# Modulation vectors of a two-layer transformer trunk: row blocks summed on VectorE, partitions on TensorE

## The chip, the cores and the metric

The kernel runs on one core of one Trainium2 chip. The metric is the device time of one execution in microseconds; the median of three runs is shown. "Modulation" means here what an adaptive norm takes from a conditioning vector: for each layer nine vectors of 1024 numbers (shift, scale and gate of three sublayers), for each of two streams.

## What is computed

Two layers work on 256 latent tokens (`x`) and 256 context tokens (`ctx`), 1024 features each. For both streams the same weights are used, but different modulation vectors, from `c` for `x` and from `c_ctx` for `ctx`:

```python
sc = jax.nn.silu(c)
scc = jax.nn.silu(c_ctx)
for l in range(DEPTH):
    mx = (sc @ w_ada[l] + b_ada[l]).reshape(bsz, N_MOD, 1, d)
    mc = (scc @ w_ada[l] + b_ada[l]).reshape(N_MOD, d)
    x = x + 0.5 * mx[2] * _swiglu(_modulate(_rmsnorm(x, norm_g[l, 0]), mx[0], mx[1]), w_ffn1_in[l], w_ffn1_out[l])
    ctx = ctx + 0.5 * mc[2] * _swiglu(...)
    hx = _modulate(_rmsnorm(x, norm_g[l, 1]), mx[3], mx[4])
    ...
    x = x + mx[5] * ox
    x = x + 0.5 * mx[8] * _swiglu(_modulate(_rmsnorm(x, norm_g[l, 2]), mx[6], mx[7]), w_ffn2_in[l], w_ffn2_out[l])
    if with_ctx:
        ctx = ctx + mc[5] * oc
        ...
return _rmsnorm(x, final_g)
```

`w_ada` is 1024 x 9216 for each layer, in fp32; the product with it is a matrix times two columns. The second layer's `ctx` is not needed behind the mixer, so of its modulations 5 to 8 only `x`'s part is used.

## The kernel before

All activations lie feature-major: eight tiles of 128 features by 512 tokens, `x` in the columns 0 to 255 and `ctx` in 256 to 511. Weights come from DRAM in blocks of 512 KB (`Unit`; four tiles of 128 rows by 256 columns), loaded by SP's queue into six buffers `wr`. ScalarE copies a block's high part into `wh` (L119), VectorE writes the rest into `wl` (L122, this pair is called the split), four buffers of each; TensorE then makes three products for each output tile and k (L110), so a block of two output tiles and four k with 512 tokens is 24 matmuls of 512 columns. A block has two parts, one for each output tile.

The feed-forward nets (FFN) take most blocks: pairs of "up" blocks (ScalarE applies silu) and "gate" blocks (VectorE multiplies from PSUM, ScalarE and VectorE split the product), then "down" blocks whose products VectorE adds to the tokens.

The modulation weights come as blocks of their own (`ada_units`, L272): for each modulation eight blocks of 128 rows by 1024 columns, called A blocks here. They are not split. `ada_product` (L242) multiplies a block with `sc` (the two silu vectors in the first two of 32 columns, one row block at a time) into one PSUM tile, in four matmuls of 256 columns, one for each group of 32 PSUM partitions; fp32 takes two instructions for each. At the eighth block VectorE turns 32x32 squares (L257), adds the bias (L122) and applies the norm's weight or the factor 0.5 into `mods`. The first two modulations of layer 0 are made in the opening (`first_ada`), with halves of 512 columns.

The program's order is written by hand. `mixed` (L1208) puts one A block behind each block of an FFN's middle: 56 in layer 0's first FFN (L1244), 56 of layer 1's in layer 0's second (L1248), eight in layer 1's first (L1250). The last eight (modulation 8 of layer 1) are `rest` (L1253): three between the last mixer output and the norm of the last FFN, the others behind every second block there (L1255). `ahead` (L1310) issues loads and splits for which there is room: a split up to four blocks ahead, a load when a `wr` buffer is over. `later` (L307) puts a function off by a number of parts. All engines run their queues in order.

Of the kernel before, what the change touches and what calls it, by code (L numbers as in the profile page):

```python
# [9 lines left out]
F32 = mybir.dt.float32  # L10
F32R = mybir.dt.float32r
U32 = mybir.dt.uint32
ACTF = mybir.ActivationFunctionType
ALU = mybir.AluOpType
# [3 lines left out]
KD = 8  # L18
# [6 lines left out]
# columns of w_mix_in  # L25
# [5 lines left out]
# columns of the float constants  # L31
# [3 lines left out]
N_STAGE, N_SPLIT = 6, 4  # weight blocks being loaded, and split  # L35
N_SLOT = 69
# of the layers' mixers: the turns between an attention item's stages, and the weights of the turns
# [8 lines left out]
class Ring:  # L46
    """Buffers of one size, handed out and given back in program order."""
# [22 lines left out]
class Unit:  # L70
    """A block of weights and the products that use it, in parts."""

    def __init__(self, src, shape, parts, split=True):
        self.src, self.shape, self.parts, self.split = src, shape, parts, split
        self.raw = self.hi = self.lo = None
        self.turned = 0  # the first columns' heads get the order (half, axis, frequency)
        self.far = False  # split far ahead, into buffers of the general ring


class Halves:  # L80
    """Two tiles of two k each, seen as one of four."""
# [14 lines left out]
def trunk_kernel(ctx: ExitStack, tc: tile.TileContext, a: dict, out: bass.AP, dbg=None):  # L96
# [11 lines left out]
    # ------------------------------------------------------------ helpers  # L108
# [3 lines left out]
    def mm3(o, lh, ll, rh, rl, start, stop):  # L112
        """(lh + ll)^T (rh + rl) in float32r passes."""
        mm(o, lh, rh, start, False)
        mm(o, lh, rl, False, False)
        mm(o, ll, rh, False, stop)
# [19 lines left out]
    # ---------------------------------------------------------- constants  # L136
# [5 lines left out]
    km = kf[:, C_TRI:C_TRI + 256].bitcast(U32)  # not 0 where a token counts  # L142
# [5 lines left out]
    nc.vector.memset(sc, 0.0)  # L148
    cols = [const.tile([128, 108], F32, name=f"cols{l}") for l in range(DEPTH)]
# [9 lines left out]
    # ------------------------------------------------------------- opening  # L159
# [41 lines left out]
    def tokens(k):  # L201
        """Tokens, feature-major: columns 0..255 are x, 256..511 are ctx."""
# [14 lines left out]
    def side_loads():  # L217
        """What only the mixers need."""
        nc.sync.dma_start(out=kf[:, 0:C_ID], in_=a["k_f"][:, 0:C_ID])
        for l in range(DEPTH):  # L220
# [13 lines left out]
            # minus lambda  # L234
# [4 lines left out]
    # ---------------------------------------------------------------- adaLN  # L239
    ada_ps = {}  # L240

    def ada_product(l, i, k, w, b0=0, nb=KD):  # L242
        """Row block k's share of modulation i of layer l, of the feature tiles b0.. (nb of them)."""
# [10 lines left out]
        if k < KD - 1:  # L254
            return
# [3 lines left out]
        m = mods[l][:, i, b0:b0 + nb]  # L259

        def wide(c0):
            c = cols[l][:, c0 + b0:c0 + b0 + nb]
            return c.rearrange("p (b o) -> p b o", o=1).to_broadcast([128, nb, 2])

        tt(m, tr[:, 0:32 * nb].rearrange("p (b r) -> p b r", r=32)[:, :, 0:2], wide(BADA + 8 * i), ALU.add)
# [5 lines left out]

    def ada_units(l, i):  # L272
        def part(k):
            return lambda u: ada_product(l, i, k, u.raw)
# [6 lines left out]
    def first_ada(b0):  # L281
        """Loads and products of what the first norm takes, for the feature tiles b0.. (4 of them)."""
# [14 lines left out]
    # ----------------------------------------------------------------- norm  # L297
# [9 lines left out]
    def later(f, parts=1):  # L307
        """Runs f after this many more parts: products whose operands are on their way."""
        put_off.append((n_part + parts, f))

    def square(m, c, x=None):
        """Adds tile m's squares in the columns c to the sums of squares."""
# [15 lines left out]
    def scale_of(c):  # L328
        """1 / rms of the tokens in the columns c."""
# [7 lines left out]
    def modulate(l, ni, ss, ks):  # L337
        """The tiles ks of the streams ss, normalised and modulated: all high parts, then the low ones."""
# [34 lines left out]
    def fm_units(w, c0, width, n, done, rh=None, kd=KD, r0=0, by_stream=False, turned=0):  # L373
        """Output features c0.. (128 or 256 of them), feature-major; done(m, psum, columns).

        by_stream: the parts are in two lists, x's and ctx's; done comes once for each when it is "twice".
        """
# [39 lines left out]
    def across(before, between, norm_of, after, n):  # L417
        """Units before a norm, the norm and units after it, stream by stream."""
# [29 lines left out]
    # ------------------------------------------------------------------ FFN  # L448
    def ffn(l, w_in, w_out, n, gi, after, by_stream=True):
        """Its first units, the others, the last ones and what follows these."""  # L450
# [51 lines left out]
    # ---------------------------------------------------------------- mixer  # L502
    def mixer(l, n):
        """n: the tokens that go on (512, or 256 when only x does)."""
# [11 lines left out]
        def rope(ps, nq):  # L516
            """Two heads, each in the order (half, axis, frequency): a turn pairs the rows p and p + 32."""
# [18 lines left out]
        def tm_units(c0, dst):  # L536
            """512 features, token-major."""
# [25 lines left out]
        def twice(dst, b, nq):  # L563
            """Each head of 64 in both halves of the partitions."""
# [11 lines left out]
        def bk_tokens():  # L576
            """Token-major keys of the GLA: [token, tile, head, 64]."""
# [43 lines left out]
        def gate_weights():  # L621
            """[rank of both directions and the bias, head, direction, 64]."""
# [14 lines left out]
        def r_done(b):  # L637
            def done(m, ps, c):
                # r sigmoid(r), with exp and ln only
# [12 lines left out]
        # ---- attention: items of stages, one stage a turn  # L652
# [13 lines left out]
        def head_norm(po, n, gcol, o, mul=None):  # L666
            """o = norm over the partitions of po, times gcol (and mul)."""
# [4 lines left out]
        def halves(q):  # L672
            """A tile of two 64s as two: [high; low] parts of the first, [low; high] of the second."""
# [8 lines left out]
        def doubled(k):  # L682
            """A tile of two 64s: for each its high part twice, and the low parts of both."""
# [9 lines left out]
        def score(o, q, m, c, kh, kl):  # L693
            """(high + low of q) high of k + high of q low of k"""
# [147 lines left out]
        def gla_items():  # L842
            items = []

            def decay(t):
                ts = slice(128 * t, 128 * t + 128)

                def s0():
                    # la: 16 times the log decays, [token, head, direction, 64]
# [31 lines left out]
            def head(h):  # L881
# [18 lines left out]
                def s1():  # L900
# [23 lines left out]
                    # the state each chunk starts from: [direction and key, chunk, value]  # L924
# [45 lines left out]
        def turns(items, lags=(0, 1, 2, 3)):  # L970
            """Turn t runs stage s of item t - lags[s], the oldest item first."""
# [13 lines left out]
        # ---- the merge  # L985
# [43 lines left out]
        def spread(units, groups):  # L1029
            """The groups' turns spread evenly over the units' parts.  # L1030

            groups: name -> (turns, weight of a turn); the units' list holds "may name" before which none of the
            group's turns may come, and "need name" by which all have come.
            """
# [52 lines left out]
        def send():  # L1087
            """The tokens wait in DRAM for their residual."""
# [42 lines left out]
        for cb in range(0, KD, 2):  # L1131
# [10 lines left out]
            else:  # the first halves of some blocks first: the last y come late  # L1142
# [26 lines left out]
    # ------------------------------------------------------------- the plan  # L1169
    fin = {"t": [], "xg": {}}  # L1170

    def to_out(m, c):
        """Tile m of the last residual: its squares, and itself back to token-major."""
# [34 lines left out]
    def mixed(units, fill, every=1):  # L1208
        """fill's items, one after each unit or after every so many."""
# [19 lines left out]
    # The first up-projection starts on the lower half of the features, while the others' modulation is loaded.  # L1229
# [37 lines left out]
    def split_unit(u, src, hi, lo):  # L1267
        """src, hi and lo: [128, k, columns]"""
# [41 lines left out]
    def ahead(upto=len(todo)):  # L1310
        """The loads (of the first units, upto) and the splits for which there is room."""
# [51 lines left out]
def constants():  # L1363
    """Rope tables, triangles, masks and the identity: of the shapes alone."""
# [42 lines left out]
```

## Time and profile before

| | |
|---|---|
| time, median of 3 runs | 2339.99 us (2339.8 to 2340.06) |
| span of the profiled execution | 2337.8 us |
| TensorE (PE) busy | 2306.1 us, 99% |
| VectorE (DVE) busy | 1133.4 us, 48% |
| ScalarE (ACT) busy | 962.9 us, 41% |
| products with `sc` behind the opening | 1024 instructions in 128 blocks |

The span runs from the first to the last instruction of one profiled execution; 2.2 us of the median lie around it. Engines are named as the profile does: PE for TensorE's matmuls, PEld for its weight loads, DVE for VectorE, ACT for ScalarE. Lengths of matmuls in a timeline overlap, since they are pipelined: the distance of two starts tells what one costs in a row. "128x512" is partitions by elements. `s_t` is any of the 69 general buffers, `p_t` a PSUM bank.

### The profile page before, as it was taken

How to read it: one execution, taken by the hardware profiler on the slowest of the kernel's cores; microseconds unless marked ns; L12 is line 12 of the kernel's file. 1: busy time of each engine (PE TensorE's matmuls, PEld its weight loads, DVE VectorE, ACT ScalarE, POOL GpSimd, SP SyncE). 2: the span in 40 equal slices, each digit the busy share in tenths (PEclk: the TensorE clock that was granted, in tenths of full speed). 3: DMA queues.
4: the chain of work that ended last, by engine and by line, in shares of the span. 5: the costliest groups of instructions: out<-in, count | busy, mean ns of one | idle time of the engine just before them, and what ended most of it. 6: DMA issues, size and time to landing. Idle time of an engine off the chain costs nothing.

```text
span 2337.8 us, 33013 instructions
## 1 busy us (share of the span) xinstructions
PE 2306.1 (99%) x13479; PEld 1878.2 (80%) x13479; DVE 1133.4 (48%) x1883; ACT 962.9 (41%) x1625; POOL 189.7 (8%) x206
## 2 busy tenths in 40 slices
PE   7999999999999999999999999999999999999998
PEld 5777777977777788887777788888889778998998
DVE  5333333767455464543323354333338655776555
ACT  4321222556555544332212233322336656665443
POOL 0000000164100010000000000000004520100000
PEclk9999999999999999999999999999999999999999
DMA  8555554341211213345555435332233323346652
GB/s 300 161 174 168 166 173 159 106 132 60 70 58 55 72 55 95 113 153 171 163 172 170 158 113 159 112 99 92 89 99 109 93 73 108 110 152 216 201 183 97
DMA packets 246647, 304.53 MB, mean 130 GB/s; under 512 B 12874, under 2 KB 218180, under 8 KB 246496
## 3 DMA queue, kind: packets, MB, share of 16 engines
q1 hardware_dynamic: 245472, 301.65, 40.8%
q8 instruction: 106, 1.74, 0.3%
q10 hardware_dynamic: 448, 0.59, 0.1%
q14 instruction: 45, 0.37, 0.0%
q0 software_dynamic: 576, 0.18, 0.0%
HBM read 298.19 MB, written 4.19 MB: 129 GB/s over the span
## 4 chain that ended last, share of the span: by engine, by line
PE 91%; DVE 3%; ACT 2%; POOL 1%; DMA 1%; issue 1%; SPq 0%; ACTq 0%; DVEq 0%; POOLq 0%
PE p_t L110 89%; ACT s_t L119 2%; DVE s_t L125 1%; PE p_t L659 1%; DMA s_t<-in_w_ada_dram 1%; DVE wl L122 1%; ACT wh L119 0%; DVE av_s L717 0%; POOL s_t L525 0%; POOL s_t L689 0%; POOL s_t L524 0%; DVE s_t L122 0%; POOL s_t L526 0%; DMA s_t<-in_ctx_dram 0%; DMA wr<-in_w_ffn_in_dram 0%
## 5 line engine op out<-in xcount | busy, mean ns | idle before, releaser
L110 PE MATMUL p_t<-s_t,wh 128*128 128x512 f32 (+1 forms) x6152 | 1671.2, 355 | 1.3 <-ACT wh L119 1.3
L110 PEld LDWEIGHTS p_t<-s_t,wh 128*128 128x128 f32 x6152 | 1084.9, 189 | 221.9 <-issue 59.8
L110 PE MATMUL p_t<-s_t,wl 128*128 128x512 f32 (+2 forms) x3076 | 1046.7, 352 | 0.6 <-DVE wl L122 0.6
L122 DVE TENSOR_TENSOR wl<-wr,wh 128x1024 fp32r<-128x1024 f32 (+2 forms) x423 | 497.7, 1183 | 804.0 <-ACT wh L119 802.7
L119 ACT ACTIVATE wh<-wr 128x1024 fp32r<-128x1024 f32 (+2 forms) x423 | 414.7, 987 | 650.5 <-PE p_t L110 577.6
L110 PEld LDWEIGHTS p_t<-s_t,wl 128*128 128x128 f32 (+1 forms) x3076 | 581.1, 189 | 76.1 <-DVE wl L122 0.9
L119 ACT ACTIVATE s_t<-s_t 128x512 fp32r<-128x512 f32 (+5 forms) x322 | 175.2, 544 | 385.0 <-DVE s_t L122 242.8
L110 PE MATMUL p_t<-s_t,s_t 128*128 128x256 f32 (+4 forms) x2040 | 298.9, 307 | 8.8 <-ACT s_t L119 5.0
L110 PEld LDWEIGHTS p_t<-s_t,s_t 128*128 128x128 f32 (+2 forms) x2040 | 234.5, 184 | 64.0 <-issue 35.1
L119 ACT ACTIVATE s_t<-p_t 128x512 f32<-128x512 f32 (+5 forms) x404 | 199.4, 511 | 194.1 <-PE p_t L110 174.9
L122 DVE TENSOR_TENSOR s_t<-s_t,s_t 128x512 fp32r<-128x512 f32 (+3 forms) x217 | 129.1, 595 | 113.6 <-ACT s_t L119 112.6
L524 POOL TENSOR_TENSOR s_t<-s_t,kf 128x256 f32<-128x256 f32 x26 | 23.9, 920 | 1410.9 <-DVE s_t L523 953.1
L122 DVE TENSOR_TENSOR s_t<-s_t,p_t 128x512 f32<-128x512 f32 (+1 forms) x144 | 85.1, 591 | 55.3 <-PE p_t L110 48.0
L110 PE MATMUL p_t<-wh,s_t 128*128 128x512 f32 x256 | 82.6, 395 | 0.0
L110 PE MATMUL p_t<-wr,sc 128*32 128x256 f32 x1024 | 81.4, 391 | 0.0
L125 DVE SCALAR_TENSOR_TENSOR s_t<-p_t,mods,s_t 128x256 f32<-128x256 f32 x136 | 61.1, 478 | 40.0 <-PE p_t L110 39.6
L125 DVE SCALAR_TENSOR_TENSOR s_t<-s_t,mods,s_t 128x256 fp32r<-128x256 f32 (+1 forms) x176 | 70.6, 478 | 10.6 <-ACT s_t L119 10.6
L110 PEld LDWEIGHTS p_t<-wh,s_t 128*128 128x128 f32 x256 | 48.1, 188 | 11.0 <-issue 1.0
L110 PEld LDWEIGHTS p_t<-wr,sc 128*32 128x32 f32 x1024 | 20.3, 108 | 43.4 <-DMA wr<-in_w_ada_dram 28.9
L110 PE MATMUL p_t<-wl,s_t 128*128 128x512 f32 x128 | 50.2, 392 | 1.0 <-DVE wl L122 1.0
L119 ACT ACTIVATE s_t<-p_t,av_s 128x512 f32<-128x512 f32 (+1 forms) x48 | 29.2, 613 | 46.1 <-DVE av_s L718 46.1
L1005 POOL TENSOR_TENSOR s_t<-s_t,s_t 128x512 f32<-128x512 f32 (+1 forms) x16 | 21.7, 1370 | 298.8 <-DVE s_t L122 298.8
(101 smaller groups left out, 836.4 us busy)
## 6 DMA issues: line engine op xcount, KB each, us to landing
wr<-in_w_ffn_in_dram SPq DMA_DIRECT2D x176, 512.0 KB, 3.5
wr<-in_w_ada_dram SPq DMA_DIRECT2D x128, 512.0 KB, 4.0
wr<-in_w_mix_in_dram SPq DMA_DIRECT2D x108, 512.0 KB, 3.7
wr<-in_w_ffn_out_dram SPq DMA_DIRECT2D x80, 512.0 KB, 3.4
s_t<-in_w_ada_dram SPq DMA_DIRECT2D x32, 256.0 KB, 6.2
wr<-in_w_mix_out_dram SPq DMA_DIRECT2D x16, 512.0 KB, 3.3
wr<-in_w_ffn_out_dram SPq DMA_DIRECT2D x16, 256.0 KB, 2.6
wr<-in_w_br_a_dram SPq DMA_DIRECT2D x8, 512.0 KB, 3.3
```

The source lines that it names most:

```text
L110: nc.tensor.matmul(o, l, r, start=start, stop=stop)
L119: nc.scalar.activation(out=o, in_=i, func=f, **kw)
L122: nc.vector.tensor_tensor(out=o, in0=x, in1=y, op=op)
L125: nc.vector.scalar_tensor_tensor(out=o, in0=x, scalar=s, in1=y, op0=op0, op1=op1)
L524: nc.gpsimd.tensor_tensor(out=r[:, 0:T], in0=r[:, 0:T], in1=sin, op=ALU.mult)
L659: nc.tensor.transpose(pt[:, 128 * t:128 * t + 128], p[:, 128 * t:128 * t + 128], ident)
L1005: nc.gpsimd.tensor_tensor(out=ys[y][:, 0:n], in0=ys[y][:, 0:n], in1=g[:, 0:n], op=ALU.add)
```

## The change

The two modulations of the opening stay. For the other 16, `ada_step` takes the place of `ada_product`: at each of the eight A blocks VectorE multiplies the block's two halves of 512 columns by the column `sc[:, k, s]` and adds them to an accumulator in SBUF, for each stream `s`. At the eighth block `ada_sum` is put off by four parts; it sums the accumulators over the partitions, by products with `pick`, a constant of ones in column 0 or 1, and hands the PSUM tile to `ada_done`, which is the old end of `ada_product`. For the modulations 5 to 8 of layer 1 only `x`'s stream is made. Comments and docstrings are removed too, which moves line numbers (L1286, the load, is L1324 after).

```diff
+    pick = const.tile([128, 2, 32], F32, name="pick")
+    nc.vector.memset(pick, 0.0)
+    for s in range(2):
+        nc.vector.memset(pick[:, s, s:s + 1], 1.0)
...
-        if k < KD - 1:
-            return
+        if k == KD - 1:
+            ada_done(l, i, ada_ps.pop((l, i)), b0, nb)
+
+    def ada_done(l, i, ps, b0=0, nb=KD, streams_=2):
         tr = S.get()
         nc.vector.transpose(out=tr[:, 0:32 * nb], in_=ps[:, 0:32 * nb])
         P.put(ps)
-        m = mods[l][:, i, b0:b0 + nb]
+        m = mods[l][:, i, b0:b0 + nb, 0:streams_]
...
+    def ada_step(l, i, k, w):
+
+        ns = 1 if l == DEPTH - 1 and i >= 5 else 2
+        if k == 0:
+            ada_acc[l, i] = [[S.get(), S.get()] for _ in range(ns)]
+        acc = ada_acc[l, i]
+        for s in range(ns):
+            eng = nc.vector
+            for hf in range(2):
+                o, x, c = acc[s][hf], w[:, 512 * hf:512 * hf + 512], sc[:, k, s:s + 1]
+                if k == 0:
+                    eng.tensor_scalar_mul(out=o, in0=x, scalar1=c)
+                else:
+                    eng.scalar_tensor_tensor(out=o, in0=x, scalar=c, in1=o, op0=ALU.mult, op1=ALU.add)
+        if k == KD - 1:
+            later(lambda: ada_sum(l, i, ns), 4)
+
+    def ada_sum(l, i, ns):
+        acc = ada_acc.pop((l, i))
+        ps = P.get()
+        for hf in range(2):
+            for s in range(ns):
+                v = acc[s][hf].rearrange("p (b g c) -> p b g c", g=4, c=32)
+                for g in range(4):
+                    mm(ps[32 * g:32 * g + 32, 128 * hf:128 * hf + 128].rearrange("p (b c) -> p b c", c=32),
+                       pick[:, s, :], v[:, :, g, :], s == 0, s == ns - 1)
+        for a_ in acc:
+            S.put(*a_)
+        ada_done(l, i, ps, streams_=ns)
+
     def ada_units(l, i):
         def part(k):
-            return lambda u: ada_product(l, i, k, u.raw)
+            return lambda u: ada_step(l, i, k, u.raw)
```

TensorE's order in layer 0's first FFN, between two blocks, before: the four matmuls of an A block stand between the last product of one block (`wh_1215`) and the first of the next.

```order
L110 MATMUL p_t_1356<-s_t_386,wh_1215 128x512
L110 MATMUL p_t_1356<-s_t_394,wh_1215 128x512
L110 MATMUL p_t_1168<-wr_1251,sc 32x256 x4
L110 MATMUL p_t_1343<-s_t_580,wh_1255 128x512
L110 MATMUL p_t_1343<-s_t_580,wl_1256 128x512
```

The same engine after, at the sum of one modulation: these stand once for eight A blocks, between the two parts of a block (`wh_1055`).

```order
L110 MATMUL p_t_1187<-s_t_390,wh_1055 128x512
L110 MATMUL p_t_1187<-s_t_398,wh_1055 128x512
L110 MATMUL p_t_1200<-s_t_843,pick 32x128 x4
L110 MATMUL p_t_1200<-s_t_845,pick 32x128 x4
L110 MATMUL p_t_1200<-s_t_844,pick 32x128 x4
L110 MATMUL p_t_1200<-s_t_846,pick 32x128 x4
L110 MATMUL p_t_1221<-s_t_373,wh_1055 128x512
```

At all other places of A blocks TensorE's products of neighbouring blocks now follow each other.

VectorE's order in the same FFN, before: a split, the gate's four operations, and the next splits.

```order
L122 TENSOR_TENSOR wl_1131<-wr_1128,wh_1130 128x1024
L122 TENSOR_TENSOR s_t_1064<-s_t_1064,p_t_1092 128x512
L122 TENSOR_TENSOR s_t_1148<-s_t_1064,s_t_1147 128x512
L122 TENSOR_TENSOR s_t_1078<-s_t_1078,p_t_1105 128x512
L122 TENSOR_TENSOR s_t_1165<-s_t_1078,s_t_1164 128x512
L122 TENSOR_TENSOR wl_1178<-wr_1175,wh_1177 128x1024
```

After: the A block's four operations stand between the splits, and the turn of the last modulation behind them.

```order
L122 TENSOR_TENSOR wl_1134<-wr_1131,wh_1133 128x1024
L122 TENSOR_TENSOR s_t_1071<-s_t_1071,p_t_1099 128x512
L122 TENSOR_TENSOR s_t_1151<-s_t_1071,s_t_1150 128x512
L122 TENSOR_TENSOR s_t_1085<-s_t_1085,p_t_1112 128x512
L122 TENSOR_TENSOR s_t_1168<-s_t_1085,s_t_1167 128x512
L291 TENSOR_SCALAR s_t_1171<-wr_1051,sc 128x512
L291 TENSOR_SCALAR s_t_1172<-wr_1051,sc 128x512
L291 TENSOR_SCALAR s_t_1173<-wr_1051,sc 128x512
L291 TENSOR_SCALAR s_t_1174<-wr_1051,sc 128x512
L122 TENSOR_TENSOR wl_1184<-wr_1181,wh_1183 128x1024
L263 STREAM_TRANSPOSE s_t_1217<-p_t_1200 128x256
```

The splits for later blocks are now queued behind the sums of an A block. VectorE's order at the norm of the last FFN, after (`s_t_17711` holds the sums of squares, `s_t_17867` and `s_t_17868` are low parts of weights, `mods_90` layer 1's modulations):

```order
L122 TENSOR_TENSOR s_t_17711<-s_t_17711,s_t_17854 128x256
L291 TENSOR_SCALAR s_t_17857<-wr_17578,sc 128x512
L291 TENSOR_SCALAR s_t_17858<-wr_17578,sc 128x512
L293 SCALAR_TENSOR_TENSOR s_t_17857<-wr_17632,sc,s_t_17857 128x512
L293 SCALAR_TENSOR_TENSOR s_t_17858<-wr_17632,sc,s_t_17858 128x512
L293 SCALAR_TENSOR_TENSOR s_t_17857<-wr_17664,sc,s_t_17857 128x512
L293 SCALAR_TENSOR_TENSOR s_t_17858<-wr_17664,sc,s_t_17858 128x512
L122 TENSOR_TENSOR s_t_17867<-wr_17536,s_t_17865 128x512
L122 TENSOR_TENSOR s_t_17868<-wr_17536,s_t_17866 128x512
L125 SCALAR_TENSOR_TENSOR s_t_17880<-s_t_17586,mods_90,s_t_17873 128x256
```

Before, TensorE had the twelve matmuls of these three A blocks at this place, and VectorE's row lacked the L291 and L293 lines; otherwise it is the same.

## Rows read from the trace of the kernel before

**Rows 1.** Page, part 1: busy us (share of the span) and instructions

```profile
PE 2306.1 (99%) x13479; PEld 1878.2 (80%) x13479; DVE 1133.4 (48%) x1883; ACT 962.9 (41%) x1625; POOL 189.7 (8%) x206
```

**Rows 2.** Page, part 4: the chain that ended last, by line

```profile
PE p_t L110 89%; ACT s_t L119 2%; DVE s_t L125 1%; PE p_t L659 1%; DMA s_t<-in_w_ada_dram 1%; DVE wl L122 1%; ACT wh L119 0%; DVE av_s L717 0%; POOL s_t L525 0%; POOL s_t L689 0%; POOL s_t L524 0%; DVE s_t L122 0%; POOL s_t L526 0%; DMA s_t<-in_ctx_dram 0%; DMA wr<-in_w_ffn_in_dram 0%
```

**Rows 3.** Instructions grouped by line and shape, TensorE: busy us, mean ns

```profile
L110 PE MATMUL p_t<-wr,sc 128*32 128x256 f32 x1024 | 81.4, 391 | 0.0
```

**Rows 4.** Timeline, all engines: start us, length us, engine, line, operation

```profile
202.02 0.64 PE L110 MATMUL p_t<-wr,sc 128*32 128x256 f32 x8
202.12 1.06 ACT L119 ACTIVATE wh<-wr 128x1024 fp32r<-128x1024 f32 x1 [5.13 <-PE p_t L110]
...
203.15 0.39 PE L110 MATMUL p_t<-s_t,wh 128*128 128x512 f32 x1
...
203.21 1.23 DVE L122 TENSOR_TENSOR wl<-wr,wh 128x1024 fp32r<-128x1024 f32 x1 [4.96 <-ACT wh L119]
...
204.54 1.30 PE L110 MATMUL p_t<-s_t,wh 128*128 128x512 f32 x5
...
205.67 0.39 PE L110 MATMUL p_t<-s_t,wl 128*128 128x512 f32 x1
...
207.03 0.39 PE L110 MATMUL p_t<-s_t,wl 128*128 128x512 f32 x1
...
208.26 0.64 PE L110 MATMUL p_t<-wr,sc 128*32 128x256 f32 x8
```

**Rows 5.** Timeline of TensorE in the opening

```profile
34.88 1.95 PE L110 MATMUL p_t<-s_t,sc 128*32 128x128 f32 x64
36.77 5.73 PE L110 MATMUL p_t<-s_t,s_t 128*128 128x512 f32 x24
42.43 1.95 PE L110 MATMUL p_t<-s_t,sc 128*32 128x128 f32 x64
```

**Rows 6.** Grouped by line and shape, VectorE: busy us, mean ns of one

```profile
L125 DVE SCALAR_TENSOR_TENSOR s_t<-s_t,mods,s_t 128x256 f32<-128x256 f32 x88 | 35.8, 478 | 10.6 <-ACT s_t L119 10.6
...
L125 DVE SCALAR_TENSOR_TENSOR s_t<-s_t,av_s,s_t 128x512 f32<-128x512 f32 x16 | 14.8, 926 | 0.6
L810 DVE TENSOR_SCALAR s_t<-s_t,cv_s 128x512 f32<-128x512 f32 x32 | 14.1, 484 | 0.6
...
L125 DVE SCALAR_TENSOR_TENSOR s_t<-p_t,subg,s_t 128x512 f32<-128x512 f32 x4 | 3.0, 751 | 2.6 <-ACT s_t L119 2.4
```

**Rows 7.** Timeline of VectorE, up and gate blocks of the first FFN

```profile
274.28 0.69 DVE L122 TENSOR_TENSOR s_t<-s_t,p_t 128x512 f32<-128x512 f32 x1 [1.13 <-PE p_t L110]
275.67 0.69 DVE L122 TENSOR_TENSOR s_t<-s_t,s_t 128x512 fp32r<-128x512 f32 x1 [0.70 <-ACT s_t L119]
...
279.34 1.23 DVE L122 TENSOR_TENSOR wl<-wr,wh 128x1024 fp32r<-128x1024 f32 x1 [0.26 <-ACT wh L119]
...
299.24 0.69 DVE L122 TENSOR_TENSOR s_t<-s_t,p_t 128x512 f32<-128x512 f32 x1 [1.16 <-PE p_t L110]
```

**Rows 8.** Stages: PE, PEld, DVE, ACT, POOL busy; PEclk, DMA share, GB/s

```profile
77.00:300.00 223.00, 223.00 (x1147) 163.82 (x1146) 70.07 (x86) 52.66 (x62) 0.00 (x0) 1.00 0.53 168
```

**Rows 9.** Timelines of TensorE and VectorE before the last norm

```profile
2122.50 1.50 PE L110 MATMUL p_t<-wr,sc 128*32 128x256 f32 x24
...
2124.09 1.29 DVE L122 TENSOR_TENSOR s_t<-wr,s_t 128x512 fp32r<-128x512 f32 x2
2125.74 2.46 DVE L125 SCALAR_TENSOR_TENSOR s_t<-s_t,mods,s_t 128x256 f32<-128x256 f32 x6 [0.36 <-ACT s_t L119]
```

**Rows 10.** Chain in order of time before the last norm: start, us, what

```profile
2123.57 0.44 DVE s_t L122
...
2129.45 5.79 PE p_t L110 x28
```

**Rows 11.** Page, part 6: DMA issues, KB each, us from issue to landing

```profile
wr<-in_w_ffn_in_dram SPq DMA_DIRECT2D x176, 512.0 KB, 3.5
...
s_t<-in_w_ada_dram SPq DMA_DIRECT2D x32, 256.0 KB, 6.2
```

More of the change, by code (lines that the diff above doesn't have):

```diff
@@ L258, in ada_product @@
         P.put(ps)
-        m = mods[l][:, i, b0:b0 + nb]
+        m = mods[l][:, i, b0:b0 + nb, 0:streams_]
         def wide(c0):
             c = cols[l][:, c0 + b0:c0 + b0 + nb]
-            return c.rearrange("p (b o) -> p b o", o=1).to_broadcast([128, nb, 2])
-        tt(m, tr[:, 0:32 * nb].rearrange("p (b r) -> p b r", r=32)[:, :, 0:2], wide(BADA + 8 * i), ALU.add)
+            return c.rearrange("p (b o) -> p b o", o=1).to_broadcast([128, nb, streams_])
+        tt(m, tr[:, 0:32 * nb].rearrange("p (b r) -> p b r", r=32)[:, :, 0:streams_], wide(BADA + 8 * i), ALU.add)
         S.put(tr)
@@ L270, in ada_product @@
             nc.vector.tensor_scalar_mul(out=m, in0=m, scalar1=0.5)
+    ada_acc = {}
+    def ada_step(l, i, k, w):
[25 more added lines that the diff above has]
+        ada_done(l, i, ps, streams_=ns)
     def ada_units(l, i):
         def part(k):
-            return lambda u: ada_product(l, i, k, u.raw)
+            return lambda u: ada_step(l, i, k, u.raw)
         return [
```

## The prediction, made before the changed kernel ran

> **What bounds the kernel now.** I read the busy times first, then the chain that ended last, then the timeline. TensorE is busy 99% of the span, VectorE 48% [rows 1], and the chain lies on TensorE's product line, L110, for 89% of the span [rows 2]. So a microsecond counts if it is taken from TensorE's row of matmuls, and work put on VectorE is free until VectorE becomes late. The reader should see in the timeline that there are no gaps to win: matmuls of 512 columns follow each other every 0.23 us, and at 202.02 and 208.26 the eight instructions of one modulation block sit between them [rows 4]. There are 1024 of those in 128 blocks of eight [rows 3], so most of the 128 blocks (call them A blocks) are direct time on the path.
>
> **What leaves TensorE.** From one A block to the next is 208.26 - 202.02 = 6.24 us [rows 4]. In between stand the 24 matmuls of one weight block (two output tiles, 4 k, three products). In a quiet stretch six of them take 207.03 - 205.67 = 1.36 us, 0.2267 each; beside VectorE's split six take 204.54 - 203.15 = 1.39 us, 0.2317 each [rows 4]. The split lasts 1.23 us, about 5.3 matmuls, so the 24 cost 18.7 x 0.2267 + 5.3 x 0.2317 = 5.47 us, and the A block 6.24 - 5.47 = 0.77 us. Of the 128 blocks three stand in the gap before the last norm, where TensorE waits anyway [rows 9, 10]; they give nothing. The others give 125 x 0.77 = **96.3 us**.
>
> **What comes to TensorE.** At the end of each of 16 modulations, products with `pick` of 128 columns. The opening has that shape: 64 instructions of 128 columns start at 34.88, and 42.43 - 34.88 = 7.55 us later the next 64, with 24 matmuls between [rows 5]. 7.55 - 24 x 0.2267 = 2.11 us for 64. An A block has a fixed part besides its instructions: three in a row show 24 instructions in 1.50 us [rows 9], the last 0.39 us long by the mean [rows 3], so one each 1.11 / 23 = 0.048 us; 0.77 - 8 x 0.048 = 0.38 us are fixed. Then one of 128 columns costs (2.11 - 0.38) / 64 = 0.027 us. A sum over both streams has 2 halves x 2 streams x 4 groups, each two instructions as now (1024 for 512 written): 32, or 0.38 + 0.86 = 1.24 us; with one stream 16, 0.81 us. Twelve modulations have two streams, four have one (5 to 8 of the last layer): 12 x 1.24 + 4 x 0.81 = **18.1 us** back.
>
> **What comes to VectorE.** For each A block four operations on 128x512 (two streams, two halves), or two with one stream. The same operation with a column scalar and 256 wide takes 0.478 us, and six in a row 2.46 us, so each further one 0.396 us [rows 6, 9]. At 512 wide it is 0.751 us [rows 6], 0.273 more, so 0.67 us in a row, 2.68 us for four. The first block of each modulation is a plain product by a scalar, 0.484 us [rows 6]. The other end is 0.926 us, for the form with two SBUF inputs and a column of a small tile [rows 6]; that one comes right after the instruction whose result it reads, while the new ones depend on a result four instructions back, so I take 0.67 and keep 0.926 for the range. None removes a VectorE operation: the turn to columns and the bias stay.
>
> **Does it hide?** The densest stretch is the FFN's up and gate blocks. Now VectorE does in four blocks (274.28 to 299.24, 24.96 us) four splits of 1.23 us and four operations of 0.69 us for the gate, with two gaps of 0.70 us in which it waits for ScalarE's copy [rows 7]. Afterwards it has 4 x (2.68 + 1.23) + 4 x 0.69 + 2 x 0.70 = 19.8 us, and TensorE 4 x 24 x 0.2317 = 22.2 us. It fits, with 2.4 us to spare. The order shows what is queued behind the sums: the splits for a block four ahead, the gate's operations, the turn of the last modulation. A split is due three blocks after it can start, some 16 us, and the sum with `pick` comes four parts after the last block, one and a half blocks or 8 us. These two are the cover; if VectorE is later than that, TensorE waits by the excess. I put no wait in the sum.
>
> **Slower matmuls beside VectorE.** 0.2317 against 0.2267 us is 2.2%. VectorE is now 70 of 223 us busy there [rows 8]; each two-stream block adds 2.68 us, so 0.058 us. 96 two-stream blocks and 29 with half as much: **6 us** lost. Bounds: nothing, if those are other causes, and 10 us.
> The Trainium skill, "SBUF — State Buffer", section "SBUF: two separate sides", speaks against such a term: "PE, ACT, and DVE's dedicated pair never wait on anyone." By that the 6 us fall away and the sum ends at 2265. The trace differs, 0.2317 beside a split and 0.2267 without, and I go by the trace.
>
> **The last norm.** There the order puts the six VectorE operations of the first three blocks of modulation 8 between the last sum of squares and the two splits and the modulation's first step. Two products and four sums: 2 x 0.48 + 4 x 0.67 = 3.6 us. Now the squares end at 2124.01 [rows 10], two splits run from 2124.09 to 2125.38, and the modulation starts at 2125.74 [rows 9], waited for by TensorE until 2129.45 [rows 10]. Then: 2124.0 + 3.6 + 1.3 = 2128.9, **3.2 us** later. The three A blocks that filled TensorE's wait are gone, so this is added to the path in full. Bounds 2 and 5 us.
>
> **DMA.** SP's queue now waits for VectorE where it waited for TensorE: the load of a weight block goes into the buffer of an A block and starts when that block's fourth sum ends. The loads are as many as before, 0.53 of the DMA time in that stretch [rows 8]; nothing is added. The six buffers hold three blocks ahead, so I cost it at nothing; the last rival says what happens if not.
>
> **Sum.** -96.3 + 18.1 + 6 + 3.2 = -69.0 us. The span of the profiled execution is 2337.8 us, 2.2 under the median of 2339.99; what lies around the span stays. 2339.99 - 69.0 = **2271 us**.
>
> **Rivals.**
> VectorE is late. If the sums cost 0.926 us, four blocks take it 19.8 + 4 x 4 x 0.256 = 23.9 us against 22.2: 1.7 us too long. There are 78 A blocks in up and gate stretches, 19.5 such rounds: 33 us if none is absorbed, 2304; with some absorbed by the 8 to 16 us of cover, 2285 to 2304. For it: margin of only 11%, and ScalarE waits in the queue. Against: the 0.478 and 0.751 rows. In the profile TensorE would wait for VectorE at `pick` or at `wl`.
> Slower: the loads bind. VectorE's sum of a block frees a buffer, the load lands, ScalarE copies (1.06 us [rows 4]), VectorE splits (1.23) and only behind that split, two blocks on, stands the next but one block's sum. So two blocks take at least the landing time + 1.06 + 1.23 + 2.68 us. With 3.5 us to landing [rows 11] that is 8.5 us, 4.2 a block, under 5.56. It decides from a landing of 7.4 us on: then a block takes 6.18 us, which over 112 blocks eats the 69 us. The opening shows 6.2 us with all loads queued at once [rows 11]. At 8 us, 6.49 a block: 2271 + 112 x 0.93 = 2375. Against: the DMA is half idle.
> The change takes less than it says: if only the instructions and not the fixed 0.38 us of a block went, 2271 + 48 = 2319. I see no reason for that, since the fixed part stands beside these blocks alone.
>
> **How the numbers follow.** Forecast 0.71 (a third of it for the case without the 6 us), VectorE late 0.20, partly freed 0.03, loads bind 0.04, no change 0.02 (0.2%, 5 us, is about what a measurement of this kernel can tell from none). The forecast's own bounds: without the 6 us and with 2 us at the norm 2264, with cheaper sums some 2259; with 10 and 5 us 2277. The range takes in the greater part of the second case: 2259 to 2300. Faster by over 0.2%: 0.71 + 0.20 + 0.03 = 0.94; same 0.02; slower 0.04.
>
> **What would show it.** Groups after: no product of `wr` and `sc`; about 450 VectorE operations on `wr` and `sc`, near 0.7 us each, VectorE's busy time up by some 285 us to about 1420; 448 TensorE instructions with `pick`. In FFN stretches with A blocks a round of four blocks takes 22 us instead of 25, and TensorE stays over 98% busy. Wrong would be: an operation of 0.9 us or more; TensorE waiting for VectorE for more than some 10 us in all; splits that wait for DMA; or a last norm that ends more than 5 us later.

## The result

The changed kernel takes 2260.8 us (median, 2260.13 to 2261.69) against 2339.89 for the kernel before on the same chip: 0.9662 of it, interval 0.9651 to 0.9674, 79.1 us less. The prediction was 2271, with a range of 2259 to 2300. Direction, cause and range hold; the gain is 10 us larger than the sum said, and the experiments below show which two of its terms were mis-sized.

### The profile after

The page's busy times, which answer to [rows 1]:

```profile
PE 2222.7 (98%) x12903; PEld 1877.4 (83%) x12903; DVE 1408.8 (62%) x2334; ACT 962.4 (43%) x1625; POOL 189.6 (8%) x206
```

TensorE has 576 instructions less (1024 gone, 448 with `pick` come in), VectorE 451 more. VectorE is 275.4 us busier and TensorE still 98% busy. The groups of the new operations (line, engine, operation, shapes, count, busy us, mean ns):

```profile
L293 DVE SCALAR_TENSOR_TENSOR s_t<-wr,sc,s_t 128x512 f32<-128x512 f32 x392 | 269.0, 745 | 0.0
...
L291 DVE TENSOR_SCALAR s_t<-wr,sc 128x512 f32<-128x512 f32 x56 | 23.5, 480 | 0.0
```

The forms that were only bounded before are thus at the near rows, 0.751 and 0.484 us [rows 6], not at 0.926. In a row they cost less, as the timeline of VectorE in the first FFN shows:

```profile
200.07 2.73 DVE L293 SCALAR_TENSOR_TENSOR s_t<-wr,sc,s_t 128x512 f32<-128x512 f32 x4
202.72 1.22 DVE L122 TENSOR_TENSOR wl<-wr,wh 128x1024 fp32r<-128x1024 f32 x1
203.85 2.73 DVE L293 SCALAR_TENSOR_TENSOR s_t<-wr,sc,s_t 128x512 f32<-128x512 f32 x4
```

Four sums and a split take 203.85 - 200.07 = 3.78 us, where 2.68 + 1.23 = 3.91 was assumed. TensorE in the same stretch:

```profile
202.02 0.39 PE L110 MATMUL p_t<-s_t,wl 128*128 128x512 f32 x1
...
204.74 0.39 PE L110 MATMUL p_t<-s_t,wl 128*128 128x512 f32 x1
...
211.77 1.07 PE L110 MATMUL p_t<-s_t,wh 128*128 128x512 f32 x4
212.76 1.08 PE L110 MATMUL p_t<-s_t,pick 128*32 128x128 f32 x32
213.78 0.50 PE L110 MATMUL p_t<-s_t,wh 128*128 128x512 f32 x1
214.11 0.40 PE L110 MATMUL p_t<-s_t,wl 128*128 128x512 f32 x1
...
215.72 0.62 PE L110 MATMUL p_t<-s_t,wh 128*128 128x512 f32 x2
```

From 202.02 to 204.74 stand twelve matmuls, 0.2267 us each, and VectorE is busy all that time. From 211.77 to 215.72 stand twelve more and the 32 instructions with `pick`: 3.95 - 12 x 0.2267 = 1.23 us for a sum over both streams (1.24 in the prediction). By the same reckoning, with the slower matmuls behind it, a sum of one stream (at 1250.72, 1292.36 and 1400.27) costs 0.84 us (0.81 in the prediction).

TensorE's waits, the longest and those for VectorE on the product line (line that waits, what it waits for, us in total, times, longest):

```profile
PE p_t L110 <- ACT s_t L119: 7.8, 3, 4.9
...
PE p_t L110 <- DVE s_t L125: 3.9, 6, 1.4
...
PE p_t L110 <- DVE s_t L122: 2.0, 2, 1.5
...
PE p_t L110 <- DVE wl L122: 1.6, 3, 0.7
```

None is for the new sums (L291, L293); the longest, 4.9 us, is the last norm. The stages, by the start of each norm's first products with `ones_d` in the two traces, show where the 79 us came from:

| from norm to norm | before, us | after, us | difference | what the change does there |
|---|---|---|---|---|
| 19.8 / 19.9 to 434.0 / 397.6 | 414.2 | 377.7 | -36.5 | 56 A blocks of two streams out, 7 sums in |
| to 982.7 / 946.3 | 548.7 | 548.7 | 0.0 | nothing (mixer) |
| to 1390.2 / 1316.9 | 407.5 | 370.6 | -36.9 | 56 A blocks out, 5 sums of two streams and 2 of one in |
| to 1759.4 / 1680.5 | 369.2 | 363.6 | -5.6 | 8 A blocks out, 1 sum of one stream in |
| to 2124.1 / 2044.7 | 364.7 | 364.2 | -0.5 | nothing (mixer) |
| to 2330.6 / 2252.0 | 206.5 | 207.3 | +0.8 | 5 A blocks out, 1 sum in, the last norm later |

The first row gives the price of an A block by itself: (36.5 + 7 x 1.23) / 56 = 0.81 us; the third, with 0.84 for a sum of one stream, (36.9 + 5 x 1.23 + 2 x 0.84) / 56 = 0.80. The prediction had 0.77.

### The profile page after: what moved, and what is told of

It is laid out like the page before. It is cut to its first block, busy times and chain, and to the rows that moved or that the text cites. A ratio compares the mean times of both kernels' runs of the same rounds, so it can differ in the third digit from the quotient of the medians.

```text
span 2259.2 us, 32395 instructions
## 1 busy us (share of the span) xinstructions
PE 2222.7 (98%) x12903; PEld 1877.4 (83%) x12903; DVE 1408.8 (62%) x2334; ACT 962.4 (43%) x1625; POOL 189.6 (8%) x206
## 4 chain that ended last, share of the span: by engine, by line
PE 91%; DVE 4%; ACT 2%; POOL 1%; issue 1%; DMA 1%; SPq 0%; ACTq 0%; POOLq 0%; DVEq 0%
PE p_t L110 89%; ACT s_t L119 2%; DVE s_t L125 1%; PE p_t L697 1%; DMA s_t<-in_w_ada_dram 1%; DVE wl L122 1%; POOL s_t L727 0%; ACT wh L119 0%; DVE av_s L755 0%; POOL s_t L563 0%; DVE s_t L122 0%; POOL s_t L564 0%; POOL s_t L562 0%; SPq L185 0%; DVE s_t L561 0%
## 5 line engine op out<-in xcount | busy, mean ns | idle before, releaser
L110 PE MATMUL p_t<-s_t,wh 128*128 128x512 f32 (+1 forms) x6152 | 1639.5, 353 | 1.6 <-ACT wh L119 1.3
L293 DVE SCALAR_TENSOR_TENSOR s_t<-wr,sc,s_t 128x512 f32<-128x512 f32 x392 | 269.0, 745 | 0.0
L122 DVE TENSOR_TENSOR s_t<-s_t,p_t 128x512 f32<-128x512 f32 (+1 forms) x144 | 85.0, 590 | 27.3 <-PE p_t L110 19.9
L110 PE MATMUL p_t<-wl,s_t 128*128 128x512 f32 x128 | 50.2, 392 | 1.0 <-DVE wl L122 1.0
L119 ACT ACTIVATE s_t<-s_t,mods 128x256 fp32r<-128x256 f32 x88 | 36.4, 496 | 12.5 <-DVE s_t L125 12.5
```

The lines of the kernel that those rows point to most:

```text
L110: nc.tensor.matmul(o, l, r, start=start, stop=stop)
L119: nc.scalar.activation(out=o, in_=i, func=f, **kw)
L122: nc.vector.tensor_tensor(out=o, in0=x, in1=y, op=op)
L293: eng.scalar_tensor_tensor(out=o, in0=x, scalar=c, in1=o, op0=ALU.mult, op1=ALU.add)
```

## The experiments

Each was timed beside the kernel before, whose median lay between 2340.1 and 2340.5 in these comparisons.

### VectorE's work alone

The kernel before, with VectorE's sums added and used by nobody (`sums`, left out of the lines below, holds the operations of `ada_step`).

```diff
...
-            return lambda u: ada_product(l, i, k, u.raw)
+            def go(u):
+                ada_product(l, i, k, u.raw)
+                sums(k, u.raw)
+            return go
```

> The kernel before, with VectorE's sums added beside TensorE's products (all modulations but the last one, whose sums would stand before the norm); the sums are not used. It asks whether VectorE's work slows TensorE's matmuls. Theory now: it does not, the slower matmuls stand behind each block of 32-column products whatever VectorE does; time within 2 us of the kernel before, 2339 to 2342, and matmuls at 0.226 us again from the ninth behind a block. Rival, my prediction's term: each of the 96 + 24 blocks costs 0.058 or 0.029 us, 6 us more, 2346. Second rival, VectorE late: over 2350, with TensorE waiting for VectorE.

Measured: 2340.06 us, ratio 1.0001 (0.9992 to 1.0011). The stretch of [rows 8] (TensorE's busy time and instructions, its weight loads', VectorE's, ...):

```profile
77.00:300.00 223.00, 223.00 (x1146) 163.93 (x1146) 158.60 (x230) 52.91 (x62) 0.00 (x0) 1.00 0.55 168
```

VectorE works 158.60 us there instead of 70.07, TensorE issues 1146 instructions instead of 1147, and nothing is longer. So VectorE's reads and writes cost TensorE's matmuls nothing here, and the prediction's 6 us for them fall. This is what the rule says that was weighed there (the Trainium skill, "SBUF — State Buffer", section "SBUF: two separate sides"); the run agrees, with 1.0001.

The slower matmuls of [rows 4], 0.2317 us, have another place. In the timeline of after above they follow the sum with `pick`: 0.33 us from the first to the second (213.78 to 214.11), then 1.61 us for the next seven, 0.230 each, and none beside VectorE's work at 202.02. In [rows 4] they stand behind the A block in the same way; that a split ran there too was a coincidence of the order. They are part of what an A block costs: 6.24 - 24 x 0.2267 = 0.80 us, and not 0.77.

### The sums left out

The kernel after, without the sums of the blocks 2 to 8.

```diff
-        for s in range(ns):
+        for s in range(ns if k == 0 else 0):
```

> The changed kernel in which VectorE makes only the first block's product of each modulation; the sums of blocks 2 to 8 are left out, all loads and the products with pick stay. It prices VectorE's whole added work. Theory now (hidden but for the last norm): 2.7 us of four sums leave the norm's chain, so 2257 to 2259. Rival, VectorE slows or delays TensorE elsewhere: 6 us and more on top, 2252 or less.

Measured: 2258.11 us, ratio 0.9649 (0.9634 to 0.9663): 392 VectorE operations of 0.745 us, 253 us of its busy time, are worth 2.7 us. By the starts of the norms all but 0.3 us of it lies behind the last one (2044.4 there, 2044.7 in after). The sums are hidden except at that place.

### The last norm

The kernel after, with the three A blocks of modulation 8 that stood before the last norm moved behind it.

```diff
-    prog += across(mx[1][2], [mx[1][3]] + rest[:3], lambda s: norm(1, 2, s, T), f2[1][0], T)
-    prog += mixed(f2[1][1], rest[3:], 2) + f2[1][2] + [f2[1][3], final]
+    prog += across(mx[1][2], [mx[1][3]], lambda s: norm(1, 2, s, T), f2[1][0], T)
+    prog += mixed(f2[1][1], rest, 2) + f2[1][2] + [f2[1][3], final]
```

> The changed kernel with the three blocks of modulation 8 that stand before the last norm moved behind it, among the last FFN's blocks. Theory: the 3.2 us that the norm's chain got longer come back, 2257 to 2258.5. Rival: the chain is held by ScalarE and the splits as well, or the blocks cost the same behind the norm, where VectorE and the splits are busy: 2260 to 2262.

Measured: 2258.07 us (2257.71 to 2258.79), ratio 0.9649 (0.9633 to 0.9665), 2.7 us under after. That is little: the times of the two kernels don't overlap, the intervals of their ratios do (0.9651 to 0.9674 for after), and they were not timed side by side. The chain shows the difference directly. First the chain of after at the norm (start us, us, what), which answers to [rows 10], and the timeline's line for its first piece, the last step of the sum of squares:

```profile
2044.26 0.04 DVE s_t L122
...
2044.60 0.88 DVE s_t L291 x2
...
2046.06 2.07 DVE s_t L293 x3
2048.13 1.20 DVE s_t L122 x2
...
2052.95 6.71 PE p_t L110 x28
```

```profile
2044.26 0.43 DVE L122 TENSOR_TENSOR s_t<-s_t,s_t 128x256 f32<-128x256 f32 x1 [0.48 <-ACT s_t L119]
```

and the same place with the three blocks moved:

```profile
2044.05 0.44 DVE s_t L122
...
2049.92 6.41 PE p_t L110 x28
```

The reader sees the two products and four sums in the chain, between the squares and the modulation's first step. The chain gives the squares' last step 0.04 us in after, as it goes on with VectorE's next instruction; the operation itself takes 0.43 us there, as in the other two. So the three are compared from its start. To TensorE's next long piece it is 2052.95 - 2044.26 = 8.69 us in after, 2129.45 - 2123.57 = 5.88 before [rows 10] and 2049.92 - 2044.05 = 5.87 here. The term is 2.81 us where 3.2 were predicted, and the 2.7 us that this run gains (3.3 between the profiled executions) are about that term.

TensorE's piece of 28 behind it is longer in after too, 6.71 against 5.79 us before, 0.9 us that no step of the prediction had. In stretches of 7.1 us from the start of the piece (before, after, and with the blocks moved) TensorE's granted clock, the third number from the end, is 0.70, 0.55 and 0.60 of full speed:

```profile
2129.45:2136.55 7.10, 7.10 (x40) 6.69 (x40) 5.05 (x10) 4.72 (x7) 0.00 (x0) 0.70 0.42 142
```

```profile
2052.95:2060.05 7.10, 7.10 (x33) 6.77 (x34) 5.06 (x10) 3.75 (x7) 0.00 (x0) 0.55 0.30 99
```

```profile
2049.92:2057.02 7.10, 7.10 (x36) 6.77 (x37) 5.06 (x10) 4.11 (x7) 0.00 (x0) 0.60 0.28 77
```

So the piece goes with the granted clock, but the length of the gap doesn't explain the clock: with the blocks moved the gap is as long as before, and 6.41 - 5.79 = 0.6 of the 0.9 us is still there; in the next run the gap is 12.13 us and the piece takes 6.14 us, at 0.65. Why the clock comes back later than before stays open.

### Two streams everywhere

The kernel after, with both streams for the modulations 5 to 8 of the last layer as well.

```diff
-        ns = 1 if l == DEPTH - 1 and i >= 5 else 2
+        ns = 2
```

> The changed kernel with both streams' sums for all 16 modulations (the single-stream part undone). Theory: VectorE's 32 blocks with two more operations, some 41 us of its time, are hidden except in the norm's chain (two products and four sums more, 3.5 us), and TensorE has four times 16 instructions more, 1.7 us: 2266. Rival, VectorE near its limit: the blocks in the second FFN add waits, 2270 or more.

Measured: 2268.57 us, ratio 0.9693 (0.9679 to 0.9708), 7.8 us more than after (6.9 between the two profiled executions), between the theory's 2266 and the rival's 2270. About half of it is the last norm, where now four products and eight sums stand. The last line, from TensorE's timeline, is the sum with `pick` of the last modulation:

```profile
2046.31 0.04 DVE s_t L122
...
2046.65 1.67 DVE s_t L291 x4
...
2048.89 4.72 DVE s_t L293 x7
...
2058.44 6.14 PE p_t L110 x28
```

```profile
2109.94 1.09 PE L110 MATMUL p_t<-s_t,pick 128*32 128x128 f32 x24 [0.90 <-DVE s_t L293]
```

2058.44 - 2046.31 = 12.13 us, 3.4 more than in after. Up to that norm the loss is 2.1 us (2046.8 against 2044.7), of which the three longer sums with `pick` there give 3 x (1.23 - 0.84) = 1.2; the two FFN stages in which they stand are longer by 0.8 and 0.4 us, so doubling VectorE's operations in these 24 blocks costs nothing more. The other 0.8 us lies in layer 0's first FFN (378.2 against 377.7) and in a mixer, where this edit changes nothing. Behind the last norm the last sum has no cover left: the distance between the long matmuls around it is 2.82 us instead of 0.78 in after, 0.4 of the 2.0 for the longer sum and the rest because TensorE waits for VectorE. With the piece of 28, 0.6 us shorter here, this makes 2.1 + 3.4 + 2.0 - 0.6 = 6.9 us. Where VectorE's row is not covered, its operations count in full; the rival of added waits holds at one sum.

### What an A block consists of

The kernel before, with its A blocks in pairs, behind every second weight block (the new `pairs`, left out below, is `mixed` with two items at a time).

```diff
...
-    prog += mixed(f1[0][1][2:], [side_loads] + ada_of(0, (2, 4, 3, 5, 7, 6, 8)))
+    prog += [f1[0][1][2], side_loads] + pairs(f1[0][1][3:], ada_of(0, (2, 4, 3, 5, 7, 6, 8)))
...
-    prog += mixed(f2[0][1], ada_of(1, (1, 0, 2, 4, 3, 5, 7)))
+    prog += pairs(f2[0][1], ada_of(1, (1, 0, 2, 4, 3, 5, 7)))
...
-    prog += mixed(f1[1][1], ada_of(1, (6,)))
+    prog += pairs(f1[1][1], ada_of(1, (6,)))
```

> The kernel before, with the 120 modulation blocks of the FFNs' middles put two by two behind every second weight block instead of one behind each (all 1024 instructions are still there; in a row of two there are 16). Theory: an A block's 0.80 us on TensorE is 8 x 0.048 = 0.38 us for its instructions and 0.42 us that belong to the change from 512-column products to 32-column products and back, the somewhat longer matmuls behind it included. Then a pair costs 0.42 + 0.77 = 1.19 us instead of 1.60; some 60 pairs give 25 us: 2315 us. Rival: each instruction costs 0.1 us wherever it stands; then nothing changes: 2340 us. Third way: the loads, which now come in a different order, make TensorE wait, which its waits would show, and the time is over 2340.

Measured: 2320.7 us, ratio 0.9917 (0.99 to 0.9933), 19.4 us less with the same instructions. The timeline of TensorE:

```profile
191.72 1.07 PE L110 MATMUL p_t<-wr,sc 128*32 128x256 f32 x16
...
203.87 1.07 PE L110 MATMUL p_t<-wr,sc 128*32 128x256 f32 x16
```

From pair to pair 203.87 - 191.72 = 12.15 us with 48 matmuls between: 12.15 - 48 x 0.2267 = 1.27 us for a pair, where two single blocks cost 1.60. The 0.33 us saved for each of 60 pairs make 20 us. So if the two blocks of a pair cost the same for their instructions, an interruption of the long products costs 0.33 us, the slower matmuls behind it included, and the eight instructions the other 0.47: 0.059 each, not 0.048. The theory holds, with a fixed part smaller than the 0.42 assumed; the rival of a price for each instruction alone falls. Of the 100 us that the A blocks cost, some 41 (125 x 0.33) went with the number of interruptions and some 59 with the instructions.

What the fixed part comes from is not shown. The expectation put it down to the change to 32-column products (weights of 32 columns, `128*32`) and back. But the trace of before has, in a mixer, a change from weights of 128 to weights of 32 columns within the split products, and elsewhere one from short products with weights of 128 columns back to long ones:

```profile
555.54 1.53 PE L110 MATMUL p_t<-s_t,wh 128*128 128x512 f32 x6
556.91 0.39 PE L110 MATMUL p_t<-s_t,wl 128*32 128x512 f32 x1
...
1882.74 0.60 PE L659 MATMUL p_t<-kf,s_t 128*128 128x128 f32 x4
1883.09 0.48 PE L110 MATMUL p_t<-s_t,wh 128*128 128x512 f32 x1
1883.41 0.40 PE L110 MATMUL p_t<-s_t,wl 128*128 128x512 f32 x1
```

The first line holds the first change (its last two matmuls have weights of 32 columns), and its six starts still lie (556.91 - 555.54) / 6 = 0.228 us apart: going to 32 columns costs nothing there (the way back is followed by products of another kind and can't be read off). And behind the short products with weights of 128 columns the first long matmul takes 1883.41 - 1883.09 = 0.32 us as well. So the change to 32 columns costs nothing by itself here, and the slower first matmul comes without it too; what makes the fixed part, the runs leave open.

### How much room VectorE has

The kernel after, with two more VectorE operations for each A block of two streams.

```diff
...
                     eng.scalar_tensor_tensor(out=o, in0=x, scalar=c, in1=o, op0=ALU.mult, op1=ALU.add)
+                    if s == 1:
+                        eng.scalar_tensor_tensor(out=ada_acc["more"][hf], in0=x, scalar=c, in1=o, op0=ALU.mult, op1=ALU.add)
...
```

> The kernel after, with two more VectorE operations for each A block of two streams (into scratch that nobody reads): six instead of four, 0.67 us each. In an up and gate stretch VectorE then has, in a round of four blocks, 4 x (4.02 + 1.23) + 4 x 0.69 + 1.4 = 25.2 us of work and waits, TensorE 4 x 24 x 0.2267 = 21.8 us. Theory: VectorE's row binds there, 3.4 us for each of some 19 rounds of four blocks, 65 us at most and 40 us if the down blocks and the four blocks of cover take up a part: 2300 to 2326 us, and TensorE waits for VectorE at wl. Rival: the cover (splits four blocks ahead) hides it, at most 2265 us, and nothing shows but VectorE busier by some 120 us.

Measured: 2314.2 us, ratio 0.9889 (0.9874 to 0.9903), 53.4 us above after and inside the theory's 2300 to 2326. But TensorE doesn't wait at `wl`, as the theory had it; it waits at `pick`. Its first wait in the list, and one such sum:

```profile
PE p_t L110 <- DVE s_t L295: 33.8, 27, 8.4
```

```profile
216.47 0.43 PE L110 MATMUL p_t<-s_t,pick 128*32 128x128 f32 x8 [1.20 <-DVE s_t L295]
217.79 0.65 PE L110 MATMUL p_t<-s_t,pick 128*32 128x128 f32 x16 [0.90 <-DVE s_t L295]
```

The products follow VectorE's last sums one by one. The distances between the long matmuls around the sixteen sums are 42 us longer in all than in after, and the twenty matmuls behind them take 10 us longer in all; these are 52 of the 53.4 us. The lack of time is where the prediction looked for it; the place where it comes out is the sum with its four parts of cover, not the split with its four blocks.

### The cover: the sum without and with more of it

First the kernel after, with the sum right behind the eighth block.

```diff
-            later(lambda: ada_sum(l, i, ns), 4)
+            ada_sum(l, i, ns)
```

> The kernel after, with the products with pick issued right behind the eighth block's VectorE sums instead of four parts later. In the trace of after VectorE ends the last sum of a modulation at 206.6 us and TensorE comes to pick at 212.76, so 6.2 us of cover were left. Four parts are one and a half to two blocks, 8 to 11 us, of TensorE's row; without them TensorE comes to pick 2 to 5 us before the sum is done. Theory: the four parts are the cover; twelve sums over two streams wait 2 to 5 us each, so 24 to 60 us: 2285 to 2320 us, with TensorE waiting for VectorE at pick. Rival: VectorE is early enough without it: 2261 us.

Measured: 2329.03 us, ratio 0.995 (0.9933 to 0.9966): 68.2 of the 79.1 us are gone, more than the 24 to 60 expected. TensorE's first wait, and one of the sums:

```profile
PE p_t L110 <- DVE s_t L293: 41.1, 21, 6.0
```

```profile
1086.63 1.07 PE L110 MATMUL p_t<-s_t,wh 128*128 128x512 f32 x4
1091.47 0.66 PE L110 MATMUL p_t<-s_t,pick 128*32 128x128 f32 x8 [3.77 <-DVE s_t L293]
1092.79 1.51 PE L110 MATMUL p_t<-s_t,pick 128*32 128x128 f32 x24 [0.67 <-DVE s_t L293]
1094.23 0.80 PE L110 MATMUL p_t<-s_t,wh 128*128 128x512 f32 x1
1094.83 0.63 PE L110 MATMUL p_t<-s_t,wl 128*128 128x512 f32 x1
...
1097.38 0.46 PE L110 MATMUL p_t<-s_t,wl 128*128 128x512 f32 x1
```

The gap between the long matmuls, 1094.23 - 1086.63 - 4 x 0.2267 = 6.7 us, is 5.6 more than the 1.1 of after. All such gaps of the sixteen sums together are 52 us longer than there. Behind the long ones matmuls start every 0.43 us instead of 0.2267 (1094.83 to 1097.38, six in 2.55 us), and the stage from 1094.2 to 1097.3 shows a granted clock of 0.50, the lower level, 1.2 GHz instead of 2.4:

```profile
1094.20:1097.30 3.10, 3.10 (x11) 2.49 (x8) 2.90 (x7) 0.00 (x0) 0.00 (x0) 0.50 0.71 186
```

Seven matmuls take 3.15 us there (1094.23 to 1097.38) instead of 1.7, so 1.5 us. Nine of the sixteen gaps are of this kind (4.1 to 8.9 us); the twenty or so matmuls behind each take 1.4 to 2.2 us longer than behind a sum of after, 16 us in all. Gaps and slower matmuls, 52 + 16, are the 68 us. In after the same sums show how narrow the cover is. The last sum of VectorE before the sum with `pick` at 386.34, by the timeline of VectorE:

```profile
383.01 2.73 DVE L293 SCALAR_TENSOR_TENSOR s_t<-wr,sc,s_t 128x512 f32<-128x512 f32 x4
```

It ends at 385.74, 0.6 us before TensorE needs it. At 1071.71 it is 1.5 us, at 212.76 it is 6.2.

Then the kernel with six operations a block (the edit of "How much room VectorE has"), and in it the sum twelve parts behind the eighth block.

```diff
-            later(lambda: ada_sum(l, i, ns), 4)
+            later(lambda: ada_sum(l, i, ns), 12 if ns == 2 else 4)
```

> Six VectorE operations for each block of two streams, as in the run with six (2314.2 us, where TensorE waited 33.8 us for VectorE at pick, and 27 times), and the products with pick of two streams twelve parts after the eighth block instead of four. Theory: VectorE is short of time by some 2 to 3.4 us in four up and gate blocks, which adds up to 20 to 34 us over the ten such rounds of an FFN; pick now has 24 us of cover and no longer waits much, and the lack shows at wl, whose cover is four blocks: 2275 to 2300 us. Rival: VectorE was only late at the sums and catches up otherwise: 2261 to 2268 us. Second rival: moving the wait gains nothing, as the lack is the same wherever it is waited for: 2305 to 2314 us.

Measured: 2311.02 us, ratio 0.9875 (0.986 to 0.989). Only 3 us come back, the second rival. TensorE's first wait, and VectorE's timeline:

```profile
PE p_t L110 <- DVE wl L122: 26.8, 17, 3.7
```

```profile
250.27 1.22 DVE L122 TENSOR_TENSOR wl<-wr,wh 128x1024 fp32r<-128x1024 f32 x1
251.41 2.07 DVE L295 SCALAR_TENSOR_TENSOR s_t<-wr,sc,s_t 128x512 f32<-128x512 f32 x3
...
255.63 1.22 DVE L122 TENSOR_TENSOR wl<-wr,wh 128x1024 fp32r<-128x1024 f32 x1
```

No sum with `pick` waits any more, and the wait is at `wl`: 26.8 of the 50.2 us above after (the others are not taken apart here). A block takes VectorE 255.63 - 250.27 = 5.36 us without a gap, TensorE 24 x 0.2267 = 5.44; nothing is left for the gate's operations. So there are two separate limits: with six operations VectorE has too little time, and moving the place where TensorE waits for it gives back 3 us only; with four it has enough, but its result comes late and needs the cover.

## Why the prediction was right, and where its sizes were off

**What leaves TensorE** was right in kind: the A blocks were direct time on the path. The size was low, 0.77 instead of 0.80 us a block, 96.3 instead of 100 us. The reading that failed is "beside VectorE's split six take" 1.39 us: the slower matmuls were put down to the split, though they stand behind the A block and are part of its price.

**Slower matmuls beside VectorE** was the other side of that error: the 6 us were added for VectorE's new work, and the first experiment shows 0. These two, 3.7 + 6 = 9.7 us, are nearly the whole of 2271 - 2260.8 = 10.2; at the norm 0.9 us more and 0.4 us less cancel in part.

**What comes to TensorE**: 1.23 and 0.84 us a sum against 1.24 and 0.81. The division behind it was not right: for A blocks, 0.38 fixed and 0.048 for an instruction, the pairs give 0.33 and 0.059; for `pick`, 0.38 and 0.027, the two sizes of sum give 0.45 and 0.025. At 32 instructions the errors cancel, which is luck.

**What comes to VectorE**: 2.68 us for four sums, 2.73 measured with the end of the last; VectorE's busy time 1408.8 against "about 1420". The value at 0.926 us never came up.

**Does it hide**: yes, and both parts of that step stood the test. By the measured rows a round of up and gate blocks is 4 x 3.78 + 4 x 0.69 + 1.4 = 19.3 us of VectorE's against 21.8 of TensorE's; two more operations a block cost 53.4 us. And the cover of four parts, on which "I put no wait in the sum" rested, is worth 68 us. What the prediction had not worked out is how little of it is left: 0.6 us at one sum, 1.5 at another. The rival of a late VectorE was worked out for sums of 0.926 us; that a sum of 0.67 us can be late too, when it is asked for too soon, it did not have. Without the four parts the time is 2329, beyond its 2285 to 2304.

**The last norm**: right in kind, 2.8 us against 3.2: from the end of the squares to the modulation's first step it is 2049.25 - 2044.69 = 4.56 us, where 3.6 + 1.3 were added up, as the operations overlap at their ends. Another 0.9 us came with a lower granted clock, which the prediction didn't have and whose cause is open.

**DMA.** The loads are slower to land, and SP's queue waits for VectorE's sums (L293, 330.5 us in all), as the rival of the loads had it. The page's part on DMA issues, which answers to [rows 11], and ScalarE's wait for these loads at the copy `wh`:

```profile
wr<-in_w_ffn_in_dram SPq DMA_DIRECT2D x176, 512.0 KB, 4.2
```

```profile
ACT wh L119 <- DMA wr<-in_w_ffn_in_dram: 185.1, 48, 6.4
```

The median landing takes 4.2 us instead of 3.5, under the 7.4 us from which the rival decided. ScalarE's copy, which before waited for these loads three times, 6.6 us in all, now does so 48 times, 185.1 us in all, but TensorE waits for `wl` no more than before (1.6 us): the cover of four blocks at the split takes it.

The new sum is -125 x 0.80 + 12 x 1.23 + 4 x 0.84 + 2.8 + 0.9 = -78.2 us, against 79.1 measured (78.6 between the two profiled executions).

## What to carry to other kernels

On an engine that never idles, small products between large ones are worth looking for: here they cost by their number and by each place where they interrupt the long ones, so putting them side by side (19 us) already helps and giving the additions to an engine with spare time helps most (79). Before such work is moved, two things have to be shown apart: that the other engine has the time in the densest stretch, and that its result is asked for late enough. The place where nothing else covers it, here one norm, gets none of the moved work: moving three blocks behind it gives 2258.1 us, 2.7 less.

## What the runs showed of the hardware

TensorE's 512-column matmuls follow each other every 0.2267 us whether VectorE works beside them or not (158.60 us of 223 busy, ratio 1.0001), but the first behind an A block takes 0.33 us and the next seven 0.23. The first takes 0.32 us behind short products with weights of 128 columns too, and going from weights of 128 to 32 columns within the split products costs nothing (0.228 us).

In the run with the sum right behind the eighth block, the granted clock behind a gap of 6.7 us was 0.50, 1.2 GHz, while matmuls were already running again; behind a gap of 2.5 us in the same run (1139.44 to 1141.91) they came at the usual distance. The length of the gap alone doesn't decide: with six operations a block, the clock behind a gap of 4.5 us was 1.00 (219.90 to 222.90) and behind one of 3.0 us 0.50 (363.80 to 366.80), both gaps with products with `pick` inside. I had not expected a wait of TensorE to cost nearly a third more than its own length (16 us beside 52).
